# A trunk layer in split float32 on one core: products with the high part first, low parts of one w_down step by accumulating transfers, and pair 19 by seven block products

## The chip, the core and the metric

The kernel runs on 1 core of one Trainium2 chip. The metric is the time of one execution on the device in microseconds (us). Before the change it is 829.84 us, the median of 3 runs (829.54 to 833.35).

## What is computed

One decoder layer on 512 tokens with 1024 channels, all in float32:

```python
u = _rmsnorm(h, norm1_g[l])
proj = u @ w_in[l]
a_glu, q, k, v, r, g_low, gate_a, gate_b = _split_cols(proj)
c = a_glu[..., :CONV_CH] * jax.nn.sigmoid(a_glu[..., CONV_CH:])
c = _causal_dwconv(c, conv_dw_w[l], conv_dw_b[l])          # width 31
c = jax.nn.silu(_layernorm(c, conv_ln_g[l], conv_ln_b[l]))
y_conv = c @ w_conv_out[l]
...
o = _gla_chunked(qh, kh, vh, gkh)                          # 4 heads, chunks of 64
...
y_gla = o @ w_gla_out[l]
merged = jax.nn.sigmoid(gate_a) * y_conv + jax.nn.sigmoid(gate_b) * y_gla
h = h + merged @ w_o[l]
u2 = _rmsnorm(h, norm2_g[l])
z = _causal_dwconv(u2 @ w_ffn_up[l], ffn_dw_w[l], ffn_dw_b[l])   # 2 x 2816 columns, width 3
h = h + (jax.nn.silu(z[..., :FFN_DIM]) * z[..., FFN_DIM:]) @ w_ffn_down[l]
return _rmsnorm(h, final_g)
```

Nearly all the arithmetic is in the matrix products with `w_in` (the column groups `w_glu`, `w_qk` = q and k, `w_v`, `w_r` and the gates), `w_conv_out`, `w_gla_out`, `w_o`, `w_ffn_up` and `w_ffn_down`.

## The kernel before, in words

**Products in three parts.** TensorE multiplies in a reduced float32 format (float32r). To keep float32's precision each operand is taken as a high part, which is the value rounded to that format, and a low part, which is what is left over. A product is then three: high by low, low by high, and high by high (`mm3`, lines 395, 396 and 397), accumulated in one bank of PSUM. A tile `mm` or `ax` is such a bank; `uh`, `ul`, `ah`, `al` and the like are the parts of activations, `whi` and `wlo` those of weights.

**How weights arrive.** `order` lists all weight tiles of the program in the order of their use; a tile is 128 partitions by 1024 floats (512 KB). `load` lets SyncE (SP) issue the read of the next one into one of 4 `raw` buffers. `split_weight` makes the parts, 4 buffers each: the high part is a cast copy by ScalarE (lines 323, 342), the low part usually `raw` minus the high part by VectorE (lines 324, 351). For the tiles in `ADDED` VectorE is spared: ScalarE writes `-raw` rounded to float32r into `wlo` (line 344), and then GpSimd (POOL) issues a transfer that reads the same weights from HBM a second time and adds them onto `wlo` (line 345). `weight` hands out the next tile and keeps `LOOK` = 2 further tiles prepared. The first half of `ADDED` is five of the value tiles of `w_glu`, all of `w_qk`, and the gates; the second are 18 tiles of `w_up`.

**Ordinary tiles.** `col_tile` makes 128 output channels for 512 tokens: 8 blocks of the inner dimension times three products, 24 products of 512 columns, in the order low weight, low activation, both high for each block.

**Seven block products.** `seven` (for `w_o` and `w_down`), `up_seven` (for tiles of `w_up`) and the start of the program make a 2 x 2 block product with seven block products in place of eight, on sums of blocks of weights and of activations. Their steps are named a11, a12, s1, n2, s4, n3 and a22. In `w_down` most steps have two weight tiles, d = 0 and d = 1, for the two halves of the inner dimension of a group. STEPS gives the order: a11 with d = 0 and 1, then a12 d = 0, s1 d = 0, a12 d = 1, s1 d = 1, then the others. A step's products for one output half (i = 0 or 1) go into one bank: `x` for a11, n2, n3, a22, `y` for s1 and s4, `z` for a12, which is an `ax` bank. The weight sums that the steps need are made while they are loaded: a tile `kept` (2 buffers) holds a11's block, and POOL issues a transfer that adds the next block onto it as soon as its parts are split (`sum_on`, line 303); the block for n3 is loaded into a `raw` buffer and summed by a second, accumulating transfer of POOL's (`add_n3`, line 270), which must wait for the load to land. In `w_down` the step a12 multiplies a block that is read as it is.

**The FFN.** There are 22 pairs of up tiles: pair i is the gate tile i and the value tile 22 + i. They come in three groups, and after each group `seven` runs `w_down` on what the group gave:

```python
GROUPS = (((0, 2), (1, 3), (4, 6), (5, 7)), ((8, 10), (9, 11), (20, 21)), ((12, 14), (13, 15), (16, 18), (17, 19)))
UP_SEVEN = (6, 7, 10, 11, 14, 15, 18)
UP_BESIDE = (1, 3, 4, 5, 9, 20, 13, 16, 17)
```

A pair in `UP_SEVEN` is made by `up_seven`, in steps of 12 products of 256 columns, with the value products of the pair before it in its group set in between (`by_parts`, the argument `beside`); its banks are copied by ScalarE (lines 1572 and others) and by VectorE (1578, 1579). The tiles of the pairs in `UP_BESIDE` are in `ADDED`. A pair's tiles then go through the width-3 convolution and the gate (VectorE lines 1378, 1386, 1392, ScalarE 1376).

**What sets the order.** TensorE, VectorE, ScalarE, GpSimd and SyncE each run their own list of instructions in a fixed order and wait for each other by semaphores. The order within each list is set when the program is built, by the framework's scheduler, which goes by its own estimates of durations. The taps of the width-31 convolution (VectorE line 813) are filled in between by `fill`, with a share of taps to each weight tile. Transfers that GpSimd issues go through one queue, those that SyncE issues through another.

Of the kernel before, what the change touches and what calls it, by code (L numbers as in the profile page):

```python
# [10 lines left out]
F32 = mybir.dt.float32  # L11
# [4 lines left out]
ALU = mybir.AluOpType  # L16
# [26 lines left out]
ET = mybir.EngineType  # L43
ADDED = {("w_glu", 2 * k) for k in (2, 3, 4, 6, 7)} | {("w_qk", m) for m in range(0, KT)}
ADDED |= {(name, m) for name in ("w_gb", "w_gla") for m in range(KT)}
UP_SEVEN = (6, 7, 10, 11, 14, 15, 18)
UP_BESIDE = (1, 3, 4, 5, 9, 20, 13, 16, 17)
ADDED |= {("w_up", j) for i in UP_BESIDE for j in (i, FT + i)}
SEVEN = {"w_o": KT // 2, "w_down": FT // 2, "w_r": KT // 2, "w_v": KT // 2}


# [27 lines left out]
def trunk_layer(ctx: ExitStack, tc: tile.TileContext, a: dict, out: bass.AP):  # L79
# [225 lines left out]
    def split_weight(between=None):  # L305
        if len(ready) < len(order):
            while len(raws) <= len(ready):
                load()
            raw = raws[len(ready)]
            name, spec = order[len(ready)]  # L310
            if name in SEVEN or name == "w_up7":
                raw = operand(name, raw, *spec) if name in SEVEN else up_operand(raw, *spec)
                n = raw.shape[-1]
                if name == "w_up7" and spec[1] == "m":
                    both = wp.tile([P, D], F32R, tag="raw", name=nm("wm"), bufs=4)
                    nc.scalar.copy(both[:, :T], raw)
                    nc.vector.tensor_tensor(both[:, T:], raw, both[:, :T].bitcast(F32), ALU.subtract)
                    ready.append((both[:, :T], both[:, T:]))
                    load()
                    return  # L320
                hi = wp.tile([P, D], F32R, tag="whi", name=nm("whi"), bufs=4)[:, :n]
                lo = wp.tile([P, D], F32R, tag="wlo", name=nm("wlo"), bufs=4)[:, :n]
                nc.scalar.copy(hi, raw)  # L323
                pace[0] = nc.vector.tensor_tensor(lo, raw, hi.bitcast(F32), ALU.subtract)  # L324
                if name in SEVEN:
                    sum_on(name, *spec)
                skipped = name in INNER and raws[len(ready)] is None
                ready.append((hi, lo))
                if not skipped:
                    load()  # L330
                return
            hi = wp.tile([P, D], F32R, tag="whi", name=nm("whi"), bufs=4)
            if order[len(ready)][0] == "w_low":
                nc.scalar.copy(hi, raw)
                if order[len(ready)][1] == 0:
                    part_lo = lambda t: t.rearrange("p (k c) -> p k c", c=P)[:, :, :RANK]
                    nc.vector.tensor_tensor(part_lo(hi), part_lo(raw), part_lo(hi.bitcast(F32)), ALU.subtract)
                ready.append((hi, None))
                load()
                return  # L340
            lo = wp.tile([P, D], F32R, tag="wlo", name=nm("wlo"), bufs=4)
            nc.scalar.copy(hi, raw)  # L342
            if order[len(ready)] in ADDED:
                pace[0] = nc.scalar.activation(lo, raw, AF.Copy, scale=-1.0)  # L344
                nc.gpsimd.dma_start(lo, a[name][spec], accum_op=ALU.add)  # L345
                ready.append((hi, lo))
                load()
                return
            if between:
                between()  # L350
            pace[0] = nc.vector.tensor_tensor(lo, raw, hi.bitcast(F32), ALU.subtract)  # L351
            ready.append((hi, lo))
            load()
# [37 lines left out]
    def mm3(acc, l, r, first, last, more=False):  # L391
# [4 lines left out]
        nc.tensor.matmul(acc, lh, rl, start=False, stop=False, **kw)  # L396
        nc.tensor.matmul(acc, lh, rh, start=False, stop=last, **kw)  # L397

    def col_tile(w, acts, acc=None, lo=0, hi=T):

        if acc is None:
            acc = mm_bank()
        for k in range(KT):
            s = slice(k * P, (k + 1) * P)
            ah, al = acts[k]
            mm3(acc[:, lo:hi], (w[0][:, s], w[1][:, s]), (ah[:, lo:hi], al[:, lo:hi]), k == 0, k == KT - 1)
        return acc

    def row_half(name, j0, n, acts, nk, done, tok_inner, middle=None):
# [856 lines left out]
    def seven(name, pairs, acts, complete, at=lambda step, i: None, fine=False):  # L1266
# [19 lines left out]
        def products(step, i, parts, lo=0, hi=T, own=None):  # L1286
            acc = bank[of[step]][i][:, lo:hi] if own is None else own[:, lo:hi]
            opens = step in ("a11", "s1", "a12") or own is not None
            for d, w in parts:
                for j, pair in enumerate(acts[2 * d : 2 * d + 2]):  # L1290
                    ah, al = (x[:, i * P : (i + 1) * P] for x in pair[step])
                    c = slice(j * T + lo, j * T + hi)

                    read = 2 * d + j == len(acts) - 1
                    mm3(acc, (ah, al), (w[0][:, c], w[1][:, c]), opens and d == 0 and j == 0, read, not opens)

        def add_to(t, n, c, x, op=ALU.add):
            nc.vector.tensor_tensor(hres[t, n][:, c], hres[t, n][:, c], x[:, c], op)  # L1298
# [287 lines left out]
    def by_parts(w):  # L1586

        acc = mm_bank()
        for k in range(KT):
            s = slice(k * P, (k + 1) * P)  # L1590
            mm3(acc, (w[0][:, s], w[1][:, s]), acts2[k], k == 0, k == KT - 1)
            yield acc

    for gi, pairs in enumerate(GROUPS):
        acts = []
# [123 lines left out]
```

## Time and profile before

| what | value |
|---|---|
| median of 3 runs | 829.84 us (829.54 to 833.35) |
| the profiled execution | 828.47 us, of which the span is 826.8 |
| TensorE busy | 813.3 us |
| weight loads into TensorE | 689.9 us (beside the products) |
| VectorE busy | 676.8 us |
| ScalarE busy | 471.0 us |
| GpSimd busy | 123.1 us |
| mean granted clock of TensorE | 0.998 |
| moved by DMA | 136.65 MB, mean 165 GB/s |

The span is the time from the first to the last instruction of the profiled execution. In rows of groups stand line, engine, operation, output <- inputs, count, then busy time in us, the mean ns of one, and the idle time of the engine just before them with what ended most of it. In a timeline the first number is the start in us from the begin of the span, the second the printed duration, and a bracket at the end gives a wait in us and what ended it. PE is TensorE, DVE VectorE, ACT ScalarE, POOL GpSimd, and SP SyncE. L395 is line 395 of the kernel. The stages lie in the span so: the input projection with the convolution from 0 to some 300, the merge and `w_o` up to 475, then the three groups of the FFN, whose `w_down` begin at about 565, 660 and 782 us.

### The profile page before, as it was taken

The numbers are of one execution on the slowest core, as the hardware profiler recorded it, in microseconds if no ns is written. First come the engines' busy times: TensorE is split into PE (matmuls) and PEld (weight loads), VectorE is DVE, ScalarE is ACT, GpSimd is POOL, SyncE is SP. The second block draws the span as 40 slices with busy tenths as digits, with TensorE's granted clock in tenths as the row PEclk, the third lists the DMA queues.
The fourth block names the chain that finished last, engine by engine and source line by source line (L and its number), as shares of the span: only waits on it lengthen the run. The fifth ranks groups of instructions, "written<-read, shape, count | busy, mean of one in ns | idle before, by whom it ended". The sixth has DMA issues, their size and how long they took to land.

```text
span 826.8 us, 11023 instructions
## 1 busy us (share of the span) xinstructions
PE 813.3 (98%) x4090; PEld 689.9 (83%) x4090; DVE 676.8 (82%) x991; ACT 471.0 (57%) x669; POOL 123.1 (15%) x144
## 2 busy tenths in 40 slices
PE   8999999999999999999999999999999999999996
PEld 7988878878888888888888898888788888988885
DVE  6898978999989889854689768789858888588896
ACT  7664546695443553359344659655446543667554
POOL 2021101311122121000001012111112111220111
PEclk9999999999999999999999999999999999999999
DMA  9999849558666578221447539356835647557562
GB/s 324 310 327 222 209 116 230 129 160 211 150 131 154 134 195 202 77 102 51 153 92 205 183 116 237 93 146 153 217 93 149 166 89 217 153 153 202 131 128 101
DMA packets 50213, 136.65 MB, mean 165 GB/s; under 512 B 4624, under 2 KB 17184, under 8 KB 50160
## 3 DMA queue, kind: packets, MB, share of 16 engines
q1 hardware_dynamic: 37456, 90.91, 31.2%
q0 software_dynamic: 12528, 44.83, 30.5%
q8 instruction: 32, 0.52, 0.3%
q10 hardware_dynamic: 176, 0.20, 0.1%
q14 instruction: 21, 0.17, 0.1%
HBM read 133.84 MB, written 6.29 MB: 169 GB/s over the span
## 4 chain that ended last, share of the span: by engine, by line
PE 78%; DVE 11%; DMA 4%; issue 3%; ACT 2%; POOL 1%; SPq 0%; POOLq 0%; ACTq 0%; DVEq 0%
PE mm L396 22%; PE mm L395 22%; PE mm L397 22%; DVE c L813 4%; PE ax L395 2%; DMA wlo<-in_w_glu_dram 2%; PE mm L663 2%; PE ax L396 2%; PE ax L397 2%; DVE wlo L324 1%; DMA kept<-rows 1%; DMA x<-in_x_dram 1%; PE ax L1137 1%; DVE tmp L1378 1%; PE ax L474 0%
## 5 line engine op out<-in xcount | busy, mean ns | idle before, releaser
L395 PE MATMUL mm<-uh,wlo 128*128 128x512 f32 (+1 forms) x636 | 237.5, 374 | 3.5 <-DMA wlo<-in_w_glu_dram 1.9
L396 PE MATMUL mm<-ul,whi 128*128 128x512 f32 (+1 forms) x636 | 234.9, 369 | 0.2 <-DVE ul L486 0.2
L397 PE MATMUL mm<-uh,whi 128*128 128x512 f32 (+1 forms) x636 | 234.5, 369 | 0.0
L813 DVE SCALAR_TENSOR_TENSOR c<-h,pp,c 128x507 f32<-128x507 f32 (+20 forms) x240 | 169.9, 733 | 2.8
L395 PEld LDWEIGHTS mm<-uh,wlo 128*128 128x128 f32 x636 | 119.9, 189 | 22.9 <-DMA wlo<-in_w_glu_dram 2.1
L397 PEld LDWEIGHTS mm<-uh,whi 128*128 128x128 f32 x636 | 119.8, 188 | 20.5
L396 PEld LDWEIGHTS mm<-ul,whi 128*128 128x128 f32 x636 | 120.1, 189 | 18.7 <-DVE ul L486 0.7
L342 ACT CAST whi<-raw 128x1024 fp32r<-128x1024 f32 x94 | 97.4, 1042 | 36.7 <-PE mm L397 29.0
L344 ACT ACTIVATE wlo<-raw 128x1024 fp32r<-128x1024 f32 x47 | 49.5, 1058 | 69.6 <-PE mm L395 65.5
L323 ACT CAST whi<-raw 128x1024 fp32r<-128x1024 f32 (+1 forms) x53 | 54.0, 1027 | 52.6 <-PE mm L397 36.1
L324 DVE TENSOR_TENSOR wlo<-raw,whi 128x1024 fp32r<-128x1024 f32 (+1 forms) x53 | 65.8, 1249 | 11.5 <-ACT whi L323 11.0
L1378 DVE SCALAR_TENSOR_TENSOR tmp<-mm,pp,tmp 128x511 f32<-128x511 f32 (+1 forms) x88 | 64.5, 742 | 12.6 <-ACT tmp L1376 12.2
L351 DVE TENSOR_TENSOR wlo<-raw,whi 128x1024 fp32r<-128x1024 f32 x47 | 56.9, 1220 | 16.7 <-ACT whi L342 16.3
L323 ACT CAST whi<-kept 128x1024 fp32r<-128x1024 f32 (+1 forms) x44 | 44.3, 1009 | 37.7 <-PE mm L397 25.6
L324 DVE TENSOR_TENSOR wlo<-kept,whi 128x1024 fp32r<-128x1024 f32 (+1 forms) x44 | 52.3, 1196 | 4.3 <-ACT whi L323 4.1
L1376 ACT ACTIVATE tmp<-mm,pp 128x512 f32<-128x512 f32 x44 | 33.3, 775 | 11.6 <-PE mm L397 11.6
L1298 DVE TENSOR_TENSOR hres<-hres,mm 128x512 f32<-128x512 f32 (+1 forms) x49 | 32.4, 670 | 2.5 <-PE mm L397 2.3
L345 POOL DMA_DIRECT2D wlo<-in_w_up_dram x18 | 15.6, 866 | 95.5 <-ACT wlo L344 77.6
L396 PE MATMUL mm<-wlo,sh 128*128 128x512 f32 x66 | 25.9, 393 | 0.0
L397 PE MATMUL mm<-whi,sh 128*128 128x512 f32 x66 | 25.7, 390 | 0.0
L395 PE MATMUL mm<-h,wlo 128*128 128x512 f32 x64 | 25.4, 397 | 0.0
L395 PE MATMUL mm<-whi,sl 128*128 128x512 f32 x66 | 25.2, 391 | 0.2 <-ACT whi L323 0.2
(361 smaller groups left out, 1635.1 us busy)
## 6 DMA issues: line engine op xcount, KB each, us to landing
raw<-in_w_up_dram SPq DMA_DIRECT2D x44, 512.0 KB, 4.4
wlo<-in_w_up_dram POOLq DMA_DIRECT2D x18, 512.0 KB, 7.4
raw<-in_w_glu_dram SPq DMA_DIRECT2D x16, 512.0 KB, 5.9
raw<-in_w_down_dram SPq DMA_DIRECT2D x15, 512.0 KB, 5.1
kept<-in_w_down_dram POOLq DMA_DIRECT2D x10, 512.0 KB, 5.3
raw<-in_w_v_dram SPq DMA_DIRECT2D x8, 512.0 KB, 6.0
rows<-in_w_r_dram SPq DMA_DIRECT2D x16, 256.0 KB, 6.4
raw<-in_w_qk_dram SPq DMA_DIRECT2D x8, 512.0 KB, 5.1
```

The lines of the kernel that those rows point to most:

```text
L323: nc.scalar.copy(hi, raw)
L324: pace[0] = nc.vector.tensor_tensor(lo, raw, hi.bitcast(F32), ALU.subtract)
L342: nc.scalar.copy(hi, raw)
L344: pace[0] = nc.scalar.activation(lo, raw, AF.Copy, scale=-1.0)
L351: pace[0] = nc.vector.tensor_tensor(lo, raw, hi.bitcast(F32), ALU.subtract)
L395: nc.tensor.matmul(acc, ll, rh, start=first, stop=False, **kw)
L396: nc.tensor.matmul(acc, lh, rl, start=False, stop=False, **kw)
L397: nc.tensor.matmul(acc, lh, rh, start=False, stop=last, **kw)
L813: nc.vector.scalar_tensor_tensor(y[:, s:], c[:, : T - s], w, y[:, s:], ALU.mult, ALU.add)
L1298: nc.vector.tensor_tensor(hres[t, n][:, c], hres[t, n][:, c], x[:, c], op)
L1376: nc.scalar.activation(z, acc, AF.Identity, bias=pp[:, PP_FB + m : PP_FB + m + 1], scale=w[2])
L1378: nc.vector.scalar_tensor_tensor(z[:, s:], acc[:, : T - s], w[j], z[:, s:], ALU.mult, ALU.add)
```

## The change

It has four parts.

1. Index 19 joins `UP_SEVEN`, so the last pair before the last `w_down` is made by `up_seven` with seven block products, and the value tile of pair 17 is spread between its steps.
2. `LOW_LAST_IN` names two value tiles of `w_glu` and the eight of `w_qk`. For these, `col_products` puts the 16 products with the high part of the weights first, and the 8 with the low part last. It takes the place of the loops in `col_tile` and in `by_parts`; tiles outside the set keep their order.
3. In `w_down`, the low part for step a12 is made as for the tiles in `ADDED`: ScalarE writes `-raw`, and an accumulating transfer that POOL issues adds the block from HBM. There are six such tiles, two in each group; one of them is of half size.
4. In `seven`, the products of step a12 are sorted so that those with the low part of the weights come last within each d. This applies to `w_o` as well.

```diff
--- before.py
+++ after.py
@@ -43,9 +43,10 @@
 ET = mybir.EngineType
 ADDED = {("w_glu", 2 * k) for k in (2, 3, 4, 6, 7)} | {("w_qk", m) for m in range(0, KT)}
 ADDED |= {(name, m) for name in ("w_gb", "w_gla") for m in range(KT)}
-UP_SEVEN = (6, 7, 10, 11, 14, 15, 18)
+UP_SEVEN = (6, 7, 10, 11, 14, 15, 18, 19)
 UP_BESIDE = (1, 3, 4, 5, 9, 20, 13, 16, 17)
 ADDED |= {("w_up", j) for i in UP_BESIDE for j in (i, FT + i)}
+LOW_LAST_IN = {("w_glu", 4), ("w_glu", 8)} | {("w_qk", m) for m in range(KT)}
 SEVEN = {"w_o": KT // 2, "w_down": FT // 2, "w_r": KT // 2, "w_v": KT // 2}
 
 
@@ -321,7 +322,12 @@
                 hi = wp.tile([P, D], F32R, tag="whi", name=nm("whi"), bufs=4)[:, :n]
                 lo = wp.tile([P, D], F32R, tag="wlo", name=nm("wlo"), bufs=4)[:, :n]
                 nc.scalar.copy(hi, raw)
-                pace[0] = nc.vector.tensor_tensor(lo, raw, hi.bitcast(F32), ALU.subtract)
+                if name == "w_down" and spec[1] == "a12":
+                    pace[0] = nc.scalar.activation(lo, raw, AF.Copy, scale=-1.0)
+                    src = block(name, spec[0], spec[2], *LOADS[spec[1]])
+                    nc.gpsimd.dma_start(lo, src, accum_op=ALU.add)
+                else:
+                    pace[0] = nc.vector.tensor_tensor(lo, raw, hi.bitcast(F32), ALU.subtract)
                 if name in SEVEN:
                     sum_on(name, *spec)
                 skipped = name in INNER and raws[len(ready)] is None
@@ -343,7 +349,7 @@
             if order[len(ready)] in ADDED:
                 pace[0] = nc.scalar.activation(lo, raw, AF.Copy, scale=-1.0)
                 nc.gpsimd.dma_start(lo, a[name][spec], accum_op=ALU.add)
-                ready.append((hi, lo))
+                ready.append((hi, lo, (name, spec) in LOW_LAST_IN))
                 load()
                 return
             if between:
@@ -396,14 +402,21 @@
         nc.tensor.matmul(acc, lh, rl, start=False, stop=False, **kw)
         nc.tensor.matmul(acc, lh, rh, start=False, stop=last, **kw)
 
+    def col_products(w, acts, acc, lo=0, hi=T):
+
+        late = [(1, 0, k) for k in range(KT)] if w[2:] and w[2] else []
+        todo = [p for k in range(KT) for p in ([(0, 0, k), (0, 1, k)] if late else [(1, 0, k), (0, 1, k), (0, 0, k)])]
+        todo += late
+        for n, (low_w, low_a, k) in enumerate(todo):
+            l, r = w[low_w][:, k * P : (k + 1) * P], acts[k][low_a][:, lo:hi]
+            nc.tensor.matmul(acc[:, lo:hi], l, r, start=n == 0, stop=n == len(todo) - 1)
+            yield n
+
     def col_tile(w, acts, acc=None, lo=0, hi=T):
-
         if acc is None:
             acc = mm_bank()
-        for k in range(KT):
-            s = slice(k * P, (k + 1) * P)
-            ah, al = acts[k]
-            mm3(acc[:, lo:hi], (w[0][:, s], w[1][:, s]), (ah[:, lo:hi], al[:, lo:hi]), k == 0, k == KT - 1)
+        for _ in col_products(w, acts, acc, lo, hi):
+            pass
         return acc
 
     def row_half(name, j0, n, acts, nk, done, tok_inner, middle=None):
@@ -1286,13 +1299,18 @@
         def products(step, i, parts, lo=0, hi=T, own=None):
             acc = bank[of[step]][i][:, lo:hi] if own is None else own[:, lo:hi]
             opens = step in ("a11", "s1", "a12") or own is not None
+            todo = []
             for d, w in parts:
                 for j, pair in enumerate(acts[2 * d : 2 * d + 2]):
-                    ah, al = (x[:, i * P : (i + 1) * P] for x in pair[step])
-                    c = slice(j * T + lo, j * T + hi)
-
-                    read = 2 * d + j == len(acts) - 1
-                    mm3(acc, (ah, al), (w[0][:, c], w[1][:, c]), opens and d == 0 and j == 0, read, not opens)
+                    a = [x[:, i * P : (i + 1) * P] for x in pair[step]]
+                    b = [x[:, j * T + lo : j * T + hi] for x in w]
+                    todo += [(n, d, a[low_a], b[low_w]) for n, (low_a, low_w) in enumerate(((1, 0), (0, 1), (0, 0)))]
+                if step == "a12":
+                    todo.sort(key=lambda p: (p[1], p[0] == 1))
+            end = parts[-1][0] == (len(acts) - 1) // 2
+            kw = {} if opens else {"skip_group_check": True}
+            for n, (_, d, l, r) in enumerate(todo):
+                nc.tensor.matmul(acc, l, r, start=opens and d == 0 and n == 0, stop=end and n == len(todo) - 1, **kw)
 
         def add_to(t, n, c, x, op=ALU.add):
             nc.vector.tensor_tensor(hres[t, n][:, c], hres[t, n][:, c], x[:, c], op)
@@ -1586,10 +1604,9 @@
     def by_parts(w):
 
         acc = mm_bank()
-        for k in range(KT):
-            s = slice(k * P, (k + 1) * P)
-            mm3(acc, (w[0][:, s], w[1][:, s]), acts2[k], k == 0, k == KT - 1)
-            yield acc
+        for n in col_products(w, acts2, acc):
+            if n % 3 == 2:
+                yield acc
 
     for gi, pairs in enumerate(GROUPS):
         acts = []
```

What it does to the lists of instructions is seen at three places. On GpSimd, at the start of the first group's `w_down`; `kept` are the tiles of a11 and its sums, `raw` the blocks of n3, `wlo` the low parts. Before:

```order
L303 DMA kept_4851<-in_w_down_dram 128x1024
L303 DMA kept_4874<-in_w_down_dram 128x1024
L270 DMA raw_5185<-in_w_down_dram 128x1024
L270 DMA raw_5208<-in_w_down_dram 128x1024
L303 DMA kept_4851<-in_w_down_dram 128x1024
L303 DMA kept_4874<-in_w_down_dram 128x1024
```

After:

```order
L304 DMA kept_4851<-in_w_down_dram 128x1024
L304 DMA kept_4874<-in_w_down_dram 128x1024
L328 DMA wlo_5069<-in_w_down_dram 128x1024
L271 DMA raw_5187<-in_w_down_dram 128x1024
L328 DMA wlo_5149<-in_w_down_dram 128x1024
L271 DMA raw_5210<-in_w_down_dram 128x1024
L304 DMA kept_4851<-in_w_down_dram 128x1024
L304 DMA kept_4874<-in_w_down_dram 128x1024
```

The transfers for the two low parts of a12 stand between the first sums onto `kept` and the sums for n3: the first (`wlo_5069`) ahead of both n3 sums, the second (`wlo_5149`) between them. The queue runs in this order.

On TensorE, in step a12 of the same `w_down`, d = 1, the first output half; `ah` and `al` are the parts of two pairs' activations. Before:

```order
L395 MATMUL ax_5119<-whi_5147,al_4892 128x512
L396 MATMUL ax_5119<-wlo_5148,ah_4891 128x512
L397 MATMUL ax_5119<-whi_5147,ah_4891 128x512
L395 MATMUL ax_5119<-whi_5147,al_5108 128x512
L396 MATMUL ax_5119<-wlo_5148,ah_5107 128x512
L397 MATMUL ax_5119<-whi_5147,ah_5107 128x512
```

After:

```order
L1313 MATMUL ax_5120<-whi_5148,al_4892 128x512
L1313 MATMUL ax_5120<-whi_5148,ah_4891 128x512
L1313 MATMUL ax_5120<-whi_5148,al_5109 128x512
L1313 MATMUL ax_5120<-whi_5148,ah_5108 128x512
L1313 MATMUL ax_5120<-wlo_5149,ah_4891 128x512
L1313 MATMUL ax_5120<-wlo_5149,ah_5108 128x512
```

The same six products stand there; the two that read `wlo` have gone from the second and fifth place to the last two.

On TensorE, at one of the two `w_glu` tiles (`mm_1121`), the beginning before:

```order
L395 MATMUL mm_1121<-uh_105,wlo_1069 128x512
L396 MATMUL mm_1121<-ul_106,whi_1068 128x512
L397 MATMUL mm_1121<-uh_105,whi_1068 128x512
L395 MATMUL mm_1121<-uh_105,wlo_1069 128x512
L396 MATMUL mm_1121<-ul_106,whi_1068 128x512
L397 MATMUL mm_1121<-uh_105,whi_1068 128x512
```

After, the end of that tile:

```order
L412 MATMUL mm_1121<-uh_107,whi_1068 128x512
L412 MATMUL mm_1121<-ul_108,whi_1068 128x512
L412 MATMUL mm_1121<-uh_107,whi_1068 128x512
L412 MATMUL mm_1121<-ul_108,whi_1068 128x512
L412 MATMUL mm_1121<-uh_105,wlo_1069 128x512 x4
L412 MATMUL mm_1121<-uh_107,wlo_1069 128x512 x4
```

Before, the tile's first product read `wlo_1069`; after, that tile is first read by the 17th of the 24 products.

## The prediction

> **What bounds the kernel now.** I read the page first, then the waits of TensorE, then the timelines where the change acts.
>
> ```profile
> span 826.8 us, 11023 instructions
> PE 813.3 (98%) x4090; PEld 689.9 (83%) x4090; DVE 676.8 (82%) x991; ACT 471.0 (57%) x669; POOL 123.1 (15%) x144
> ...
> PE mm L395 <- DMA wlo<-in_w_glu_dram: 1.9, 2, 1.7
> PE mm L395 <- DMA wlo<-in_w_qk_dram: 1.6, 1, 1.6
> ...
> PE ax L395 <- ACT mm L1572: 0.5, 1, 0.5
> ```
>
> TensorE is busy 98% of the span. All its waits for weights are 1.9 + 1.6 us, so a change wins by fewer columns or by these 3.5 us, and any new wait of TensorE goes straight onto the end. The profiled execution took 828.47 us, 1.67 over its span and 1.37 under the median of 829.84; I add to the median what I find in the trace.
>
> The price of a product is the spacing of starts, not the printed duration, which overlaps the next:
>
> ```profile
> 738.79 0.40 PE L395 MATMUL mm<-uh,wlo 128*128 128x512 f32 x1
> ...
> 744.25 0.28 PE L395 MATMUL ax<-uh,wlo 128*128 128x256 f32 x1
> ...
> 745.69 0.40 PE L395 MATMUL mm<-uh,wlo 128*128 128x512 f32 x1
> ```
>
> Between the first two rows stand 24 products of 512 columns: 5.46 / 24 = 0.2275 us each. Between the last two, 12 of 256: 1.44 / 12 = 0.12 us.
>
> **High part first in w_glu tiles 4 and 8 and in w_qk.** The same 24 products in another order cost nothing. The low part is now needed 16 x 0.2275 = 3.6 us after the tile begins.
>
> ```profile
> 106.38 0.50 PE L395 MATMUL mm<-uh,wlo 128*128 128x512 f32 x1 [1.69 <-DMA wlo<-in_w_glu_dram]
> ...
> 183.56 0.50 PE L395 MATMUL mm<-uh,wlo 128*128 128x512 f32 x1 [1.60 <-DMA wlo<-in_w_qk_dram]
> ...
> 212.66 0.83 PE L1156 MATMUL ax<-ident,o 128*128 128x128 f32 x3 [0.17 <-DVE o L1150]
> ...
> 100.00:120.00 20.00, 18.31 (x81) 14.85 (x80) 18.18 (x26) 6.99 (x8) 1.77 (x3) 1.00 0.42 86
> 160.00:180.00 20.00, 20.00 (x90) 16.53 (x90) 19.64 (x32) 17.27 (x24) 2.57 (x3) 1.00 0.50 138
> 180.00:200.00 20.00, 18.40 (x92) 15.25 (x91) 19.79 (x37) 11.44 (x14) 3.43 (x4) 1.00 0.96 234
> ```
>
> 3.6 us covers both waits. (In the last three rows the columns are PE, PEld, DVE, ACT, POOL, the granted clock.) What is kept differs. Around 106 DVE has room (18.18 of 20), and the later work there follows TensorE, so the 1.9 us of the two w_glu waits are gained. From 160 to 200 DVE is full (19.64 and 19.79 of 20), and at 212.66 TensorE waits for DVE already; 1.6 us gained at 183 would be waited for there. I take **-1.9**; ends: 0, if DVE does not follow, and -3.5, if it follows for both.
>
> **Pair 19 by seven block products.** Before, its two tiles are 48 x 0.2275 = 10.92 us; after, 7 steps of 1.44 = 10.08: -0.84. The extra work is one more high and low part and the half tile (ACT and DVE), two sums on DVE, two on POOL, four copies of banks on ACT and two on DVE. The stretch where it falls is the last row below; the row above it is the end of the first group, where pair 7 in seven products runs into w_down in the same way:
>
> ```profile
> 541.00:565.00 24.00, 23.55 (x148) 20.80 (x147) 22.38 (x31) 14.13 (x22) 4.32 (x4) 1.00 0.45 115
> 757.00:781.80 24.80, 24.80 (x118) 20.77 (x118) 21.39 (x31) 13.57 (x18) 1.73 (x2) 1.00 0.69 181
> ...
> 558.55 0.38 PE L395 MATMUL ax<-n3h,wlo 128*128 128x256 f32 x1 [0.45 <-ACT mm L1572]
> ```
>
> There the work fits with one wait of 0.45 us at the step n3, behind a full DVE (22.38 of 24). I expect the same wait after: -0.84 + 0.45 = **-0.4** (ends -0.84 and +0.5). The gain of final_g now waits on SP until n3 has let go of its tile; it is read some 15 us later, and costs nothing itself.
>
> **Low parts of a12 in w_down by transfer.** There are six (two in each of three groups; one of them half size).
>
> ```profile
> L344 ACT ACTIVATE wlo<-raw 128x1024 fp32r<-128x1024 f32 x47 | 49.5, 1058 | 69.6 <-PE mm L395 65.5
> ...
> L324 DVE TENSOR_TENSOR wlo<-raw,whi 128x1024 fp32r<-128x1024 f32 (+1 forms) x53 | 65.8, 1249 | 11.5 <-ACT whi L323 11.0
> ...
> L345 POOL DMA_DIRECT2D wlo<-in_w_up_dram x18 | 15.6, 866 | 95.5 <-ACT wlo L344 77.6
> ...
> DMA to landing us min/median/max: 5.1/7.0/11.9
> ```
>
> DVE loses 5.5 x 1.25 = 6.9 us, ACT gains 5.5 x 1.06 = 5.8 us, POOL 6 x 0.87 = 5.2 us of issuing, the transfers 2.75 MB. No wait of TensorE in w_down ends at a DVE low part, so DVE's relief wins nothing; ACT and POOL have room. The price is that a low part which was ready 1.25 us after its high part now comes by a transfer of 5.1 us or more (last row, all low parts that come this way). The first group:
>
> ```profile
> 565.01 0.40 PE L395 MATMUL mm<-whi,yl 128*128 128x512 f32 x1
> ...
> 570.02 0.39 PE L396 MATMUL ax<-wlo,ah 128*128 128x512 f32 x1
> ...
> 576.85 0.39 PE L396 MATMUL ax<-wlo,ah 128*128 128x512 f32 x1
> ...
> 562.39 1.05 ACT L323 CAST whi<-raw 128x1024 fp32r<-128x1024 f32 x1 [1.76 <-PE mm L397]
> ...
> 559.56 0.88 POOL L303 DMA_DIRECT2D kept<-in_w_down_dram  x1 [12.84 <-DVE wlo L324]
> 561.65 0.86 POOL L303 DMA_DIRECT2D kept<-in_w_down_dram  x1 [1.22 <-DVE wlo L324]
> 572.33 0.87 POOL L270 DMA_DIRECT2D raw<-in_w_down_dram  x1 [9.81 <-PE mm L397]
> ...
> kept<-in_w_down_dram POOLq DMA_DIRECT2D x1, 512.0 KB, 5.3
> ...
> kept<-in_w_down_dram POOLq DMA_DIRECT2D x1, 512.0 KB, 6.6
> ...
> raw<-in_w_down_dram POOLq DMA_DIRECT2D x1, 512.0 KB, 7.2
> ```
>
> By the new order the first low product is the 23rd after 565.01: 565.01 + 22 x 0.2275 = 570.02; that of the second block is the 53rd: 576.84. The first low part: ACT can begin when a buffer is free, about 562.3, so POOL issues at about 563.6. Alone it lands at 563.6 + 5.3 = 568.9. But the two sums ahead of it landed at 559.56 + 5.3 = 564.9 and 561.65 + 6.6 = 568.2, 3.4 us apart, so behind them it lands at 571.6: a wait of 1.6.
>
> The second block stands on POOL behind the sum for n3, whose issue is at 572.33 since its own load lands late; so it is issued at 573.2 at the earliest, though its low part is ready on ACT by 570. Alone it lands at 573.2 + 5.1 = 578.3; behind that sum, at 572.33 + 7.2 + 3.4 = 582.9. Against 576.84, the group's loss is 1.5 to 6.1 us in all (the first wait is inside it). I take **+5.5**, near the upper end, since the row of two issued close together is the nearer one; 0.6 off because the load that shared the 7.2 us now starts earlier.
>
> ```profile
> 672.82 0.39 PE L396 MATMUL ax<-wlo,ah 128*128 128x512 f32 x1
> ...
> 677.81 0.39 PE L397 MATMUL ax<-whi,ah 128*128 128x512 f32 x1
> ...
> 660.88 0.85 POOL L303 DMA_DIRECT2D kept<-in_w_down_dram  x1 [5.58 <-DVE wlo L324]
> 670.29 0.88 POOL L270 DMA_DIRECT2D raw<-in_w_down_dram  x1 [8.57 <-DVE tmp L1378]
> ...
> raw<-in_w_down_dram POOLq DMA_DIRECT2D x1, 512.0 KB, 5.2
> ```
>
> Second group: the up tiles of pair (20, 21) lie between, so the first low part is issued by about 664 and needed at 672.82: hidden. The second, of half size, is issued after the sum of 670.29, which lands at 675.5; half of 3.4 later is 677.2, needed at 677.8: **0** (up to 1). Third group: POOL has both low parts ahead of the sums for n3, so only the first one's wait is left, 0 to 1.6 and a little more beside the late gain: **+1.3**.
>
> Sum: -1.9 - 0.4 + 5.5 + 0 + 1.3 = **+4.5**: 829.84 + 4.5 = **834.3 us** (0.54% slower; 0.5%, or 4.15 us, is about what a measurement here can tell from no change).
>
> **A page weighed.** The Trainium skill, "DMA: Bandwidth & Descriptors", section "Anatomy of one DMA", gives 2.0 us plus bytes / 436e3 for a transfer issued by GpSimd: by that estimate 3.2 us for 512 KB, the first low part is there at 566.8, nothing waits in it, and the sum is nearer -2. The accumulating transfers here show 5.1 us at the least, so I do not go by it.
>
> **Rivals.** *The transfers are hidden* (not slower): the place is the second block of the first group. If the queue costs it nothing it lands at 578.3 and the group loses 1.5; with no wait in the others, -1.9 - 0.4 + 1.5 = -0.8: 829.0. For it: TensorE never waited for the 18 low parts of w_up. Against: a w_up tile lasts 5.46 us, a block of w_down half of that. It decides from a landing before 582.2 on, where the sum falls under 4.15. *DVE gives nothing back at 106*: 834.3 + 1.9 = 836.2; the full rows from 160 on speak for it, the 18.18 against. *The clock falls in the long wait*: the second wait of the first group is 5.5 - 1.6 = 3.9 us; if that made TensorE run at half speed for some 3.4 us afterwards, 1.7 us more: 836.0. The rows with 1.6 to 1.7 us of waiting show 1.00 granted, and no longer wait is in the trace. The Trainium skill, "TensorE: Matmul & The Clock Gate", Part 1, says the clock is halved after an idle window of about 3.4 us; by that rule this case comes only if a whole window falls inside the wait.
>
> **How the numbers follow.** My forecast 0.62 (own range 831.5 to 836.8, from the ends of the largest term); two thirds of it lie over 4.15: 0.40 slower, 0.22 same. Transfers hidden 0.20: 0.18 same, 0.02 faster. DVE 0.10 and clock 0.08, both slower. So slower 0.58, same 0.40, faster 0.02. The range 828.0 to 838.0 takes in most of the hidden case (829.0 with its one wait, 827.5 with none) and, above, 836.2 with the upper ends of the first and the third group (0.6 and 1.2); what lies outside is little over 1 in 10.
>
> **What would show it.** The waits at w_glu and w_qk are gone, and that for DVE near 211 is longer, 1.5 to 2. New waits of TensorE for wlo of in_w_down: about 1.6 and 4 in the first group, none over 1 in the second, 1 to 2 in the last. A wait for ACT at n3 of pair 19. I am wrong if the first group's second low part lands within 6 us of its issue, or if TensorE does not wait for it at all.

## The result, and the profile after

The changed kernel takes 835.99 us in the median of 6 runs (835.61 to 839.4), the kernel before 830.62 on the same chip (6 runs): a ratio of 1.0071, 95% interval 1.0043 to 1.0098. It is slower by 0.7%, some 5.9 us by the ratio (the two medians alone differ by 5.4); forecast were 4.5, and the time lies in the range. The profiled execution took 838.44 us, with a span of 836.7; it is one of the longer ones, and that of before (828.47) is shorter than any of the six. The head of the page, and TensorE's waits:

```profile
span 836.7 us, 11137 instructions
PE 815.4 (97%) x4126; PEld 692.9 (83%) x4126; DVE 674.9 (81%) x991; ACT 479.6 (57%) x681; POOL 130.3 (16%) x152
```

```profile
PE ax L1313 <- DMA wlo<-in_w_down_dram: 9.0, 4, 4.8
PE ax L1169 <- DVE o L1163: 1.5, 1, 1.5
PE mm L676 <- ACT whi L348: 1.3, 1, 1.3
```

The 3.5 us of waits for `w_glu` and `w_qk` are gone, 1.3 of them have come back as a longer wait for VectorE (`o`), a wait for ScalarE at the start of the program (the third row) is 0.6 longer than the 0.7 of before, and four new waits for the low parts of `w_down` make 9.0 us. Here they are in the timeline of TensorE, two in the first group, one in each of the others:

```profile
570.78 0.72 PE L1313 MATMUL ax<-wlo,ah 128*128 128x512 f32 x2 [1.66 <-DMA wlo<-in_w_down_dram]
582.73 1.22 PE L1313 MATMUL ax<-wlo,ah 128*128 128x512 f32 x2 [4.84 <-DMA wlo<-in_w_down_dram]
686.78 0.50 PE L1313 MATMUL ax<-wlo,ah 128*128 128x512 f32 x1 [0.96 <-DMA wlo<-in_w_down_dram]
796.61 0.73 PE L1313 MATMUL ax<-wlo,ah 128*128 128x512 f32 x2 [1.52 <-DMA wlo<-in_w_down_dram]
```

The list of GpSimd in the first group, ScalarE's part of the second low part (the second fence), the landing of its transfer (the third: 9.2 us after the issue at 573.52), and the stretches around it (length, TensorE, weight loads, VectorE, ScalarE, GpSimd, granted clock, DMA share, and GB/s moved):

```profile
562.54 0.87 POOL L328 DMA_DIRECT2D wlo<-in_w_down_dram  x1 [1.11 <-ACT wlo L326]
572.88 0.84 POOL L271 DMA_DIRECT2D raw<-in_w_down_dram  x1 [9.47 <-DMA raw<-in_w_down_dram]
573.52 1.10 POOL L328 DMA_DIRECT2D wlo<-in_w_down_dram  x1
```

```profile
567.34 1.06 ACT L326 ACTIVATE wlo<-raw 128x1024 fp32r<-128x1024 f32 x1 [1.17 <-PE mm L1313]
```

```profile
wlo<-in_w_down_dram POOLq DMA_DIRECT2D x1, 512.0 KB, 9.2
```

```profile
575.00:581.00 6.00, 2.89 (x13) 2.06 (x11) 4.28 (x6) 1.26 (x2) 1.22 (x2) 1.00 1.01 187
581.00:588.00 7.00, 5.27 (x12) 4.18 (x13) 2.14 (x3) 0.00 (x0) 0.12 (x1) 0.52 0.68 130
588.00:590.00 2.00, 2.00 (x10) 1.64 (x9) 1.06 (x2) 1.54 (x2) 0.00 (x0) 0.96 0.00 0
```

GpSimd stands 9.47 us before the sum for n3, until that block's own load lands, and the low part stands behind it: ScalarE has written its part by 567.34 + 1.06 = 568.4, and the transfer is issued at 573.52. In the middle stretch the clock is 0.52. Stretches of 1 us show that it falls at 581.3, still inside the wait of 4.84 us, and is full again at 588.2. TensorE's products behind the wait, two of them and the first at the old pace:

```profile
584.17 0.63 PE L1313 MATMUL ax<-whi,ah 128*128 128x512 f32 x1
584.60 0.63 PE L1313 MATMUL ax<-whi,al 128*128 128x512 f32 x1
...
588.32 0.39 PE L1313 MATMUL mm<-whi,sh 128*128 128x512 f32 x1
```

They start 0.43 us apart in place of 0.2275, and the 13 products from 582.73 to 588.32 take 5.59 us in place of 2.96: 2.6 more. So the second low part of the first group alone costs 4.84 + 2.6 = 7.4 us in this execution. The waits (9.0 + 1.3 + 0.6 - 3.5) and these 2.6 make 10.0 us, smaller terms left out; the spans of the two profiled executions differ by 9.9.

### The profile page after: what moved, and what is told of

The parts are those of the page before. It is cut to its first block, busy times and chain, and to the rows that moved or that the text cites. A ratio compares the mean times of both kernels' runs of the same rounds, so it can differ in the third digit from the quotient of the medians.

```text
span 836.7 us, 11137 instructions
## 1 busy us (share of the span) xinstructions
PE 815.4 (97%) x4126; PEld 692.9 (83%) x4126; DVE 674.9 (81%) x991; ACT 479.6 (57%) x681; POOL 130.3 (16%) x152
## 4 chain that ended last, share of the span: by engine, by line
PE 73%; DVE 12%; DMA 7%; issue 4%; ACT 3%; POOL 1%; POOLq 0%; SPq 0%; ACTq 0%; DVEq 0%
PE mm L412 44%; PE mm L1313 11%; DVE c L826 4%; DMA wlo<-in_w_down_dram 3%; PE mm L676 2%; PE mm L403 2%; PE mm L402 2%; PE mm L401 2%; PE ax L1313 2%; DVE wlo L330 2%; DMA raw<-in_w_v_dram 2%; PE ax L401 1%; PE ax L402 1%; PE ax L403 1%; DMA raw<-in_w_up_dram 1%
## 5 line engine op out<-in xcount | busy, mean ns | idle before, releaser
L412 PE MATMUL mm<-ul,whi 128*128 128x512 f32 (+1 forms) x592 | 220.9, 373 | 0.2 <-DVE ul L499 0.2
L412 PE MATMUL mm<-uh,whi 128*128 128x512 f32 (+1 forms) x592 | 220.3, 373 | 0.0
L412 PE MATMUL mm<-uh,wlo 128*128 128x512 f32 (+1 forms) x592 | 210.8, 376 | 0.0
L412 PEld LDWEIGHTS mm<-uh,whi 128*128 128x128 f32 x592 | 111.5, 188 | 19.8
L412 PEld LDWEIGHTS mm<-ul,whi 128*128 128x128 f32 x592 | 111.8, 189 | 17.6 <-DVE ul L499 0.6
L412 PEld LDWEIGHTS mm<-uh,wlo 128*128 128x128 f32 x592 | 111.6, 189 | 17.3 <-DMA wlo<-in_w_glu_dram 0.2
L324 ACT CAST whi<-raw 128x1024 fp32r<-128x1024 f32 (+1 forms) x56 | 57.2, 1027 | 52.4 <-PE mm L1313 14.6
L357 DVE TENSOR_TENSOR wlo<-raw,whi 128x1024 fp32r<-128x1024 f32 x45 | 54.5, 1220 | 16.4 <-ACT whi L348 16.0
L412 PE MATMUL mm<-h,whi 128*128 128x512 f32 x128 | 39.4, 389 | 0.0
L412 PEld LDWEIGHTS mm<-h,whi 128*128 128x128 f32 x128 | 24.0, 188 | 5.2 <-issue 0.2
```

The costliest lines, as they stand in the source:

```text
L412: nc.tensor.matmul(acc[:, lo:hi], l, r, start=n == 0, stop=n == len(todo) - 1)
```

## The experiments

Each ratio is to the kernel before, run beside it; it is not the quotient of the two medians in its row. "Clock" is a figure worked out for all executions of a kernel: (1 - mean granted clock) x span, averaged. It is 2.3 to 3.0 us for the kernel before, and at the least 1.4 (glu_only). It also counts low clock where it costs nothing: in the profiled execution of before the clock falls only at 823.7, when TensorE has no product left. So what a kernel loses by the clock is at most what its figure has above some 1.4.

| kernel | median us | of before | ratio (95%) | clock us |
|---|---|---|---|---|
| the change | 835.99 | 830.62 | 1.0071 (1.0043 to 1.0098) | 4.2 |
| a12_dve | 830.42 | 831.59 | 0.9986 (0.9966 to 1.0007) | 2.4 |
| a12_only | 843.80 | 831.59 | 1.0156 (1.0114 to 1.0197) | 7.0 |
| second_on_dve | 834.19 | 831.59 | 1.0036 (1.0019 to 1.0053) | 3.9 |
| n3_behind | 833.34 | 831.59 | 1.0015 (0.9996 to 1.0033) | 3.3 |
| glu_only | 828.56 | 832.22 | 0.9948 (0.9929 to 0.9966) | 1.4 |
| qk_only | 832.78 | 832.22 | 1.0006 (0.9988 to 1.0023) | 2.8 |
| early_only | 829.28 | 832.22 | 0.9957 (0.9941 to 0.9974) | 1.8 |
| pair19_only | 834.71 | 832.22 | 1.0029 (1.0012 to 1.0045) | 2.8 |
| queue_order | 831.70 | 832.14 | 0.9992 (0.9972 to 1.0011) | 1.8 |
| third_only | 830.76 | 832.14 | 0.9972 (0.9951 to 0.9994) | 1.5 |
| no_early | 839.59 | 831.00 | 1.0111 (1.0078 to 1.0145) | 4.9 |

### The transfers for a12, taken away and alone

`a12_dve`:

```diff
-                if name == "w_down" and spec[1] == "a12":
+                if False:
```

> The changed kernel with the low parts of a12 made on VectorE again (the products of a12 stay sorted, the other parts of the change stay). Theory: all four waits of TensorE for low parts of w_down (9.0 us in the changed kernel's trace) and the halved clock behind the longest are gone; what is left is the gain of the early tiles (3.5 us less the 1.3 us given back to VectorE at 211) and of pair 19 (0.84): 2 to 3.5 us faster than before. Rival: the waits come from somewhere else in w_down (the loads of the raw blocks, which land at 570.9 and 572.1), then waits of over 1 us in w_down stay and it is not faster than before.

All four waits are gone, and the clock figure is that of before. So they, and the clock, come from the transfers: 1.0071 - 0.9986 is 0.85%, 7.1 us (give or take 2.8, by the two intervals). But it is not the 2 to 3.5 us faster that the theory gave; its waits tell where some of the rest went:

```profile
PE ax L1169 <- DVE o L1163: 1.5, 1, 1.5
PE ax L401 <- ACT mm L1584: 1.4, 1, 1.4
...
PE mm L1313 <- DVE hres L1316: 1.0, 1, 1.0
```

`a12_only` is the kernel before with the transfers and the sorted products of a12; against the changed kernel:

```diff
-UP_SEVEN = (6, 7, 10, 11, 14, 15, 18, 19)
+UP_SEVEN = (6, 7, 10, 11, 14, 15, 18)
...
-LOW_LAST_IN = {("w_glu", 4), ("w_glu", 8)} | {("w_qk", m) for m in range(KT)}
+LOW_LAST_IN = set()
```

> The kernel before with the low parts of a12 by transfer, and the a12 products sorted, alone. Theory: waits of TensorE for low parts of w_down of about 1.6 and 4.5 us in the first group, 0 to 1 in the second, 1 to 2 in the third, and some 2 to 3 us at a halved clock; 7 to 12 us slower than before, which is more than the whole change. Rival: the waits are caused by the earlier start that the other parts give; then it is under 5 us slower.

1.56% is 13 us: slower than the whole change by far, as the theory said, and a little past its upper bound. The first group's waits are 2.1 and 2.5 us, and the clock falls behind both; the surprise is the third group (GpSimd, then TensorE):

```profile
798.48 0.84 POOL L271 DMA_DIRECT2D raw<-in_w_down_dram  x1 [8.17 <-DMA raw<-in_w_down_dram]
799.18 1.02 POOL L328 DMA_DIRECT2D wlo<-in_w_down_dram  x1
```

```profile
809.13 1.22 PE L1313 MATMUL ax<-wlo,ah 128*128 128x512 f32 x2 [3.51 <-DMA wlo<-in_w_down_dram]
```

Without pair 19 the scheduler puts the sum for n3 ahead of the second low part there too, and the first group's loss happens twice, with the halved clock. In the changed kernel both low parts of the third group stand ahead of those sums, because pair 19 has moved the order.

### The place on GpSimd, and the wait behind it

`second_on_dve` leaves the transfer of that one block out; `n3_behind` keeps all six and puts the n3 sums behind them:

```diff
-                if name == "w_down" and spec[1] == "a12":
+                if name == "w_down" and spec[1] == "a12" and spec[::2] != (GROUPS[0], 1):
```

> The changed kernel, but the second of the first group's two low parts of a12 is made on VectorE; the other five still come by transfer. Theory: the wait of 4.8 us goes, that of 1.7 stays, and no slice of the span shows a clock under 0.9 in w_down: 5 to 8 us faster than the changed kernel, about as fast as before. If the fall of the clock has nothing to do with that wait, a clock near 0.5 stays for some us near 585 and the gain is 4.8 at most.

```diff
-                add_n3(name, pairs, d)
+                low = low_sent.get((name, pairs))
+                if low is None:
+                    add_n3(name, pairs, d)
+                else:
+                    with tc.issue_after(low.ins):
+                        add_n3(name, pairs, d)
...
-                    nc.gpsimd.dma_start(lo, src, accum_op=ALU.add)
+                    low = nc.gpsimd.dma_start(lo, src, accum_op=ALU.add)
+                    if spec[2] == 1:
+                        low_sent[name, spec[0]] = low
```

(`low_sent` begins as an empty dictionary.)

> The changed kernel with the same six transfers, but on GpSimd the sums for n3 stand behind both low parts of a12. Theory (the place in GpSimd's list): the second low part is issued at about 568.5 in place of 573.5, lands at 574 to 575 and is needed at 578: no wait for it, and the clock stays: 5 to 8 us faster than the changed kernel; the sums for n3 still land in time. Rival (the accumulating transfer is slow here in itself, 9 us from issue to landing): it lands at 577 to 578 with a wait of 0 to 1, or if it also delays the sums for n3, a new wait of TensorE for whi at n3 of 1 to 3 us appears.

In both the wait of 4.8 us is gone, and in `n3_behind` with the transfer still there, so its place in GpSimd's list was the cause. It is issued at 570.74 and takes 7.3 us, but is not waited for; the sums for n3 are not waited for either. The gain over the changed kernel is 2.9 us for `second_on_dve` and 4.7 for `n3_behind` by the ratios, each give or take some 2.7, where 5 to 8 were expected and the profiled execution lost 7.4. Two things fit a smaller gain: the clock of the six executions of the changed kernel, 0.993 to 0.997, shows that they do not all lose the same by it; and the waits for the first low parts are left, which can cost the clock as well. The stretch behind that wait, in `n3_behind` (wait 1.95 us) and in `second_on_dve` (2.22):

```profile
572.00:577.00 5.00, 4.00 (x11) 3.14 (x12) 2.37 (x4) 1.36 (x2) 0.86 (x1) 0.66 1.04 306
```

```profile
572.00:577.00 5.00, 3.21 (x14) 2.64 (x15) 3.61 (x6) 1.66 (x3) 0.84 (x1) 1.00 0.67 244
```

After the shorter wait the clock was 0.66 over 5 us (1.7 us lost), after the longer one 1.00. In `second_on_dve` it fell elsewhere, at 211.7, behind a wait of 1.47 us for VectorE's `o`; in `qk_only` it fell behind the same wait of 1.48, and in the five other profiled kernels that have this wait it did not. So a wait of 1.5 to 2.2 us may halve the clock or not; behind each of the longer ones (2.45, 3.12, 3.51 twice and 4.84 us, in four traces) it fell. In all the traces the low clock then lasted 3.4 us, or twice that. The Trainium skill, "TensorE: Matmul & The Clock Gate", Part 1, has the clock judged over free-running windows of about 3.4 us; these lengths agree with it, and so does it that waits of nearly one length have two outcomes. The page's table has the clock fall after an idle window: that fits the changed kernel, where TensorE's last product before the wait ends at 577.9 and the clock falls at 581.3, but not `n3_behind`, where a wait of 1.95 us sufficed.

### The early tiles

`glu_only`, `qk_only` and `early_only` are the kernel before with `col_products`, and each with its own set:

```diff
+LOW_LAST_IN = {("w_glu", 4), ("w_glu", 8)}
...
+LOW_LAST_IN = {("w_qk", m) for m in range(KT)}
...
+LOW_LAST_IN = {("w_glu", 4), ("w_glu", 8)} | {("w_qk", m) for m in range(KT)}
```

> The kernel before with the high parts first in the two w_glu tiles alone. Theory: the wait of 1.69 us at 106 goes and is kept to the end, no other wait of TensorE grows by over 0.4: 1.3 to 1.9 us faster than before. Rival (VectorE, which lags from 160 on, takes it back): the wait for VectorE at 211 grows from 0.2 to 1.5 or more, and it is as fast as before.

> The kernel before with the high parts first in the eight w_qk tiles alone. Theory: the wait of 1.60 us at 184 goes, but the wait for VectorE at 211 grows from 0.2 to 1.5 or more: within 0.5 us of before. Rival: the wait at 211 stays under 0.5 and it is 1.3 to 1.6 us faster.

> The kernel before with the high parts first in both, w_glu and w_qk, alone. Theory: 3.5 us of waits go, 1.3 come back at 211 (as in the changed kernel's trace): 1.5 to 2.2 us faster than before. Rival: the stretch from 543 to 558, where ScalarE's copies wait behind VectorE, takes up more of it by a longer wait for ScalarE's copy at the step a12 of pair 7 (1.4 us in the run with a12 on VectorE): under 1 us faster.

What is kept and what is given back came as forecast: `qk_only` is as fast as before, and its wait for VectorE at `o` is 1.5 us. `early_only` is no faster than `glu_only`. But `glu_only` gains 0.52%, 4.3 us by the ratio, where 1.3 to 1.9 were expected, and `early_only` 3.6 where 1.5 to 2.2 were. A second profile of the kernel before shows how more can be lost at the `w_glu` tiles:

> The kernel before once more, for a second profile of it. Theory (its usual execution loses more at the w_glu tiles than the profiled one): the two waits there are 2.5 to 3 us in place of 1.9, and the time is 830 to 833. Rival: the waits are 1.9 again, and what differs from execution to execution is elsewhere.

TensorE at the second of the two `w_glu` tiles, and the stretch around it:

```profile
110.10 0.79 PE L395 MATMUL mm<-uh,wlo 128*128 128x512 f32 x1 [3.51 <-DMA wlo<-in_w_glu_dram]
```

```profile
108.00:117.00 9.00, 6.90 (x18) 5.47 (x19) 4.43 (x7) 0.00 (x0) 0.00 (x0) 0.62 0.01 4
```

This execution took 835.93 us, which is past the 830 to 833 expected; the wait at the `w_glu` tile is 3.51 us in place of 1.69. The clock is 0.62 over the 9 us, and the 14 products from 110.10 to 116.12 take 6.02 us in place of 3.19: another 2.8. So the wait for this transfer changes from execution to execution, and a long one halves the clock. This is one of the long executions, not the usual one: in six traces with the old order of these tiles (before, before_again, pair19_only, qk_only, a12_only, no_early) the two `w_glu` waits together are 1.7 to 4.3 us, 2.7 in the mean, and the clock fell there in this one alone. The mean wait of 2.7 and the clock, at most 3.0 - 1.4 = 1.6 us by the table, come to about the 4.3 that `glu_only` gains; this is worked out from the traces and the table, and no run shows the two apart. With the tile's low products last the times lie within 2.8 us (828.01 to 830.8), those of before within 7 (829.34 to 836.29).

### Pair 19

`pair19_only` is the kernel before with one index more:

```diff
-UP_SEVEN = (6, 7, 10, 11, 14, 15, 18)
+UP_SEVEN = (6, 7, 10, 11, 14, 15, 18, 19)
```

> The kernel before with pair 19 by seven block products alone. Theory: 36 products of 512 columns' worth becomes shorter by 0.84 us, no wait at its n3, and the start of the last w_down waits for VectorE or ScalarE by 0.5 to 1.4 in all (1.0 and 0.2 in the run with a12 on VectorE): between 0.4 us faster and 0.5 slower than before, not to be told from no change. Rival: the last w_down has no such wait: 0.8 faster, or the sums for the four tiles delay w_down by over 2 us.

It is 0.29% slower, 2.4 us, where between 0.4 faster and 0.5 slower was expected. Two landmarks and the end, in before and in this kernel: the first product of pair 18's last step (it reads `wm`), the first and the last product of the last `w_down`:

```profile
758.56 0.28 PE L395 MATMUL mm<-uh,wm 128*128 128x256 f32 x1
...
781.78 0.39 PE L395 MATMUL mm<-whi,yl 128*128 128x512 f32 x1
...
819.89 0.28 PE L397 MATMUL ax<-whi,ah 128*128 128x256 f32 x1
```

```profile
761.86 0.28 PE L401 MATMUL mm<-uh,wm 128*128 128x256 f32 x1
...
784.36 0.40 PE L1313 MATMUL mm<-whi,yl 128*128 128x512 f32 x1
...
804.84 0.73 PE L1313 MATMUL mm<-whi,sl 128*128 128x512 f32 x2 [1.03 <-DVE hres L1316]
805.79 0.73 PE L1313 MATMUL mm<-whi,sl 128*128 128x512 f32 x2 [0.22 <-ACT whi L324]
...
824.54 0.28 PE L1313 MATMUL ax<-whi,ah 128*128 128x256 f32 x1
```

Up to `w_down` the pair takes 22.50 us in place of 23.22, 0.72 less: the products are cheaper, as worked out. The `w_down` behind it takes 40.18 us in place of 38.11. It waits for VectorE to read a bank into `hres`, since VectorE is full over its first 20.48 us, in before and here:

```profile
781.78:802.26 20.48, 20.48 (x92) 16.97 (x91) 19.43 (x27) 10.34 (x14) 3.47 (x4) 1.00 0.60 129
```

```profile
784.36:804.84 20.48, 19.45 (x87) 15.46 (x85) 20.39 (x32) 10.40 (x16) 2.58 (x3) 1.00 0.69 176
```

VectorE has 32 instructions there in place of 27, and 20.39 us of work in 20.48. Counted from start to start, the two waits and the products right behind them take 1.8 us over the usual spacing, most of the 2.07 that this `w_down` is longer. Net it is +1.35 from landmark to landmark and +2.4 by the times; what makes the rest is open. (-3.6 of `early_only` and +2.4 make -1.2, which is what `a12_dve` has, the two together with the sorted products of a12; so the sorting shows no effect of its own.)

### The parts together, and a mended order

The ratios of the parts alone, early_only, pair19_only and a12_only, add up to 1.42% slower, 12 us; the change is 0.71%. `no_early` asks which two of them meet:

```diff
-LOW_LAST_IN = {("w_glu", 4), ("w_glu", 8)} | {("w_qk", m) for m in range(KT)}
+LOW_LAST_IN = set()
```

> The changed kernel without the first part: w_glu and w_qk in the old order of products; pair 19 and the transfers for a12 stay. Theory (pair 19 puts both low parts of the third group ahead of the sums for n3 on GpSimd, and the transfers take low parts off VectorE, which pair 19 fills): with the transfers pair 19 is a gain; the last w_down lasts about 40 us from its first to its last product, not 43.5 as with the transfers alone, and the time is 1.011 to 1.013 of before, under the 1.0156 of the transfers alone. Rival (the parts add): 1.0156 + 0.0029, 1.0185 of before.

1.0111, as the theory said, and the 1.0185 of the rival lies outside the interval. By the two ratios pair 19 gains 0.45%, 3.7 us, with the transfers, where alone it costs 2.4. The intervals of `no_early` and `a12_only` overlap, so a gain is not shown by the times; that pair 19 does not cost there what it costs alone, is. From the first to the last product its last `w_down` takes 830.38 - 790.27 = 40.1 us, that of `a12_only` 837.12 - 793.67 = 43.5.

`queue_order` builds on `n3_behind` and moves the first low part ahead of the second sum onto `kept`:

```diff
+                    else:
+                        with tc.issue_after(low.ins):
+                            sum_on(name, spec[0], "a11", 1)
...
-                if name in SEVEN:
+                if name in SEVEN and (name != "w_down" or spec[1:] != ("a11", 1)):
```

> The changed kernel with the same six transfers, in another order on GpSimd: the first low part of a12 ahead of the second sum onto kept, the second ahead of both sums for n3. Theory (each transfer in GpSimd's queue lands 3.3 to 4.5 us behind the one before it): in the first group the first low part lands at about 567 to 568 where it is needed at 569, so no wait of TensorE for low parts of w_down over 0.5 us is left, and the clock doesn't fall; since the last w_down loses its wait for VectorE (1.0 at hres with all low parts on VectorE), it is 2 to 4 us faster than before, 0 to 2 faster than with a12 on VectorE. Rival (a transfer takes 8 us here wherever it stands): waits of 1 to 2 us for the first low parts stay, and it is no faster than with the sums for n3 behind.

GpSimd's issue of the first low part of the first group, its landing, and TensorE's waits in that `w_down`:

```profile
565.02 0.86 POOL L334 DMA_DIRECT2D wlo<-in_w_down_dram  x1 [3.22 <-ACT wlo L332]
```

```profile
wlo<-in_w_down_dram POOLq DMA_DIRECT2D x1, 512.0 KB, 7.1
```

```profile
572.18 0.74 PE L1324 MATMUL ax<-wlo,ah 128*128 128x512 f32 x2 [0.59 <-DMA wlo<-in_w_down_dram]
579.84 0.50 PE L1324 MATMUL ax<-whi,al 128*128 128x512 f32 x1 [0.98 <-DVE al L1421]
```

The theory is half right. The wait falls from 1.95 to 0.59, and the clock figure to 1.8, but the transfer itself takes 7.1 us, though it is issued when the one before it is nearly through. SP's load of another block runs beside it, and the second sum onto `kept` is issued 0.6 us behind it; which of them slows it is not shown. And the time that TensorE gains there it waits for VectorE's `al` a little later. The kernel is as fast as before, and no faster than `a12_dve`.

`third_only` keeps the transfers in the last group, where VectorE is full:

```diff
-                if name == "w_down" and spec[1] == "a12":
+                if name == "w_down" and spec[1] == "a12" and spec[0] == GROUPS[-1]:
...
-LOW_LAST_IN = {("w_glu", 4), ("w_glu", 8)} | {("w_qk", m) for m in range(KT)}
+LOW_LAST_IN = {("w_glu", 4), ("w_glu", 8)}
```

> High parts first in the two w_glu tiles alone, pair 19 by seven block products, and the low parts of a12 by transfer in the third group alone, in that same order on GpSimd. Theory (pair 19 costs 2 us in the last w_down because VectorE is full there, and taking 2.5 us of low parts off it frees that): the wait for hres at 803 is under 0.4 and the last w_down lasts 38.1 to 38.6 us from its first to the last product: 4.0 to 5.5 us faster than before, 0 to 0.7 faster than the two w_glu tiles alone. Rival: pair 19's copies and sums, not the low parts, fill VectorE, the wait at hres stays at 1: slower than the w_glu tiles alone by 1 to 2.

TensorE's waits in the last `w_down`:

```profile
788.33 0.73 PE L1324 MATMUL ax<-wlo,ah 128*128 128x512 f32 x2 [0.84 <-DMA wlo<-in_w_down_dram]
795.51 0.50 PE L1324 MATMUL ax<-whi,al 128*128 128x512 f32 x1 [0.52 <-DVE al L1421]
```

The wait at `hres` is gone, so the low parts did fill VectorE, and in its place stand a wait for the low part and one for `al`, activations of the last pairs. But this `w_down` still takes 822.75 - 782.32 = 40.4 us from its first to its last product, not the 38.1 to 38.6 expected, and the kernel is 0.28% faster than before, 2.3 us, not 4.0 to 5.5. So taking the low parts off VectorE did not take away what pair 19 costs. The two `w_glu` tiles alone gain 0.52%, though the two intervals overlap. No run shows that pair 19 is worth having in either form; `glu_only` has the lowest ratio of all, is faster than both kernels that were given, and cannot be told from `early_only`.

## Why the prediction was right, and where only by its sum

**What bounds the kernel.** Right: TensorE's waits and the halved clock add up to the difference of the two profiled executions (10.0 and 9.9 us). ScalarE's and GpSimd's added work cost no time that could be measured: `queue_order`, which has all six transfers in a better order, is at 0.9992, `a12_dve` without them at 0.9986.

**The early tiles, -1.9.** The mechanism was right in both halves: the gain at `w_glu` is kept, that at `w_qk` goes to VectorE (1.48 us at 211; 1.5 to 2 were named). The size was off: -4.3 us by `glu_only`, -3.6 with the `w_qk` tiles, which win nothing. The term took its wait from one profiled execution, where the two `w_glu` waits were 1.9 us (2.7 in the mean of six traces), and left out the clock behind the longer ones. That the profiled execution lay 1.37 us under the median was said, and not followed up.

**Pair 19, -0.4.** Alone it is +2.4 us. The saving of 0.84 is there (0.72 measured); the step that failed is the place of its cost. No wait for ScalarE came at its n3 in `pair19_only` (one of 0.42 us in `n3_behind`); the cost is in the `w_down` behind it, 2.07 us longer, where VectorE was full at 19.43 of 20.48 us. Its added work on VectorE was listed but given no price, and the row read for it ended before that stage.

**The transfers for a12, +5.5, 0 and +1.3.** The waits came where they were named, 1.6 and about 4 in the first group, none over 1 in the second, 1 to 2 in the last: 1.66 and 4.84, 0.96, 1.52. The cause, a transfer behind another's wait on GpSimd, is shown by `n3_behind`. The landing within 6 us that would have refuted it did not come: it took 9.2. (The row of before names a product of TensorE as what ended GpSimd's wait of 9.81 us, and the forecast put it down to the block's own load; the changed kernel's row names that load.) The price of 6.8 was for waits alone, and too low for that: they are 9.0 us in the profiled execution. By `a12_dve` the transfers cost 7.1, give or take 2.8; these hold a loss by the clock that was not in the 6.8, and VectorE's wait in the last `w_down` is taken away in exchange. That the two figures come so near is luck.

**The rivals.** The falling clock was given 0.08 as a case of its own, and comes on top of the forecast: 2.6 us in the profiled execution, at most 1.8 on average over `a12_dve` (4.2 less 2.4). That the gain at 106 would be lost as well is refuted by `glu_only`; that the transfers are hidden, by the four waits.

**The sum.** The runs make a chain: -3.6 for the early tiles (`early_only`), +2.4 for pair 19 (`pair19_only`), together the -1.2 of `a12_dve`, and +7.1 for the transfers: +5.9. Forecast were -1.9, -0.4 and +6.8: +4.5. The errors are -1.7, +2.8 and +0.3; the first two point opposite ways for reasons of their own, so that the sum is nearer than its terms is luck too.

## What to carry to other kernels

A transfer that is issued by an engine in order lands not when its data could, but after the wait of whatever stands ahead of it in that engine's list: read the list, and put what waits longest last. On an engine that is busy 98% of the span, the price of a wait of 1.5 us or more is the wait and, in some executions, 1.7 to 2.8 us of halved clock behind it; a saved wait is worth that much too, and one profiled execution shows only one of the outcomes. A part's effect can be another with a second part present, since both move the same order, so the parts alone do not add up to the whole: 1.42% against 0.71% here.

## What was not expected of the hardware

The clock fell to half after waits of 1.47, of 1.95 and of 4.84 us, and not after one of 2.22, and stayed there for 3.4 us in the first two cases (1.7 us lost in the second) and 6.8 in the third (2.6 lost, since part of it lay inside the wait). An accumulating transfer of 512 KB that GpSimd issued took 7.1 us with the one before it nearly landed, and 9.2 behind another one. A wait costs a little more than is printed, since the printed wait begins at the end of a duration that overlaps the next product: at the wait of 1.52 us at 796.61 the starts lie 1.91 us apart, 1.68 over the usual spacing, and the last `w_down` of the changed kernel lasts 39.95 us, 1.84 more than the 38.11 of before.
